# Softmax over rows with stores moved to another DMA queue: six of eight stores issued by GpSimd, one packet for each DMA engine's share

## The chip, the cores and the metric

The kernel runs on one core of a Trainium2 chip. The core has several engines that run side by side, each with its own stream of instructions: VectorE (DVE in the profile), ScalarE (ACT), GpSimd (POOL), SyncE (SP) and TensorE, which this kernel doesn't use. Data moves between main memory and the on-chip buffer by DMA. A DMA is issued by an instruction of SP, ACT or POOL, is split over 16 DMA engines, and signals a semaphore when all shares have landed. The metric is the device time of one execution in microseconds (us); lower is better. Between runs of this kernel it varies by about 0.1%.

## The reference: what is computed

A softmax with temperature 0.5 over the last axis of 16 x 1024 rows of 512 numbers:

```python
batch, seq, dim = 16, 1024, 512
x = np.random.randn(batch, seq, dim).astype(np.float32)

def reference(x):
    temp = 0.5
    x_scaled = x / temp
    x_max = np.max(x_scaled, axis=-1, keepdims=True)
    exp_x = np.exp(x_scaled - x_max)
    return (exp_x / np.sum(exp_x, axis=-1, keepdims=True)).astype(np.float32)
```

The input is 33.55 MB and so is the output. Each is moved once.

## The kernel before

The 16,384 rows are cut into 8 tiles, numbered 0 to 7 here as the variable `c` numbers them. A tile has 128 partitions with `G = 16` rows of 512 float32 each: 32 KB that lie together in main memory for each partition, 4 MB for the tile. `data` has six buffers (`BUFS = 6`): tiles 0 to 5 have one each, tile 6 takes over the buffer of tile 0 and tile 7 that of tile 1. So the load of tile 6 has to wait until the store of tile 0 has landed, and that of tile 7 until the store of tile 1 has.

All loads are issued by SP (line 66). Tile 0 is loaded in two parts, 4 rows and 12 rows of each partition; the others whole. All stores are issued by ACT (line 119), one for each tile. SP's DMAs are queue q1 in the profile and ACT's are q10. Both queues are served by the same 16 DMA engines; each partition's 32 KB of a 4 MB transfer are one packet in the records.

The work goes in 11 blocks (`blocks`): three for tile 0, one each for tiles 1 to 6, two for tile 7. For a block:

- `shift` (lines 68 to 78): DVE takes the maximum of each row, negated (line 74, which waits for the load), and doubles it (line 78). The result is the bias of the exponentials.
- `exponentials` (line 85): ACT computes exp(2x + bias) in place, one instruction for each of the 16 rows of a partition, with the row's sum.
- `scale_vector` (lines 100 and 102): DVE takes the reciprocals of the sums and multiplies all but an eighth of the rows by them, in place.
- `scale_scalar` (line 111): ACT scales the last eighth of the rows, two instructions for a whole tile.
- `store` (line 119): ACT issues the tile's store after its last block.

The order is written out by hand (the schedule is manual), and each engine runs its instructions in that order. In step `i` of the last loop ACT gets the exponentials of block i+1, the scaling of block i and its store. DVE gets the scaling of block i and then the maximum of block i+2. So in the middle of the run, DVE alternates between the multiplication for one tile (line 102) and the maximum of the tile two further on (line 74). A store of tile c comes after the exponentials of tile c+1 in ACT's order. Waits on semaphores are put in by the framework from the data that each instruction touches.

Tile 7's two blocks are the tail: maximum and exponentials of its first half, then of its second half, the two multiplications, and the last store.

Of the kernel before, what the change touches and what calls it, by code (L numbers as in the profile page):

```python
# [1 line left out]

# [4 lines left out]


@with_exitstack
def kernel(  # L10
    ctx: ExitStack,
    tc: tile.TileContext,
    x: bass.AP,
    out: bass.AP,
):
    nc = tc.nc
    fp32 = mybir.dt.float32
    P = nc.NUM_PARTITIONS
    AX = mybir.AxisListType.X
    EXP = mybir.ActivationFunctionType.Exp  # L20
    COPY = mybir.ActivationFunctionType.Copy
    MAX = mybir.AluOpType.max

    D = x.shape[-1]
    xf = x.flatten_outer_dims()
    of = out.flatten_outer_dims()
    N = xf.shape[0]

    G = 16
    C = N // (P * G)
    assert C * P * G == N
    xr = xf.rearrange("(c p g) d -> c p g d", p=P, g=G)
    outr = of.rearrange("(c p g) d -> c p g d", p=P, g=G)
    WHOLE = [(0, G)]
    LOADS = [[(0, 4), (4, G)]] + [WHOLE] * 7
    BLOCKS = [[(0, 4), (4, 8), (8, G)]] + [WHOLE] * 6 + [[(0, 8), (8, G)]]
    STORES = [WHOLE] * 8  # L40
    BMAX = 16
    BUFS = 6

    data = ctx.enter_context(tc.tile_pool(name="data", bufs=BUFS))
    stats = ctx.enter_context(tc.tile_pool(name="stats", bufs=6))

    ctx.enter_context(tc.manual_schedule())


    warm = stats.tile([P, 1], fp32, name="warm", bufs=1)  # L50
    nc.vector.memset(warm, 0.0)  # L51
    nc.scalar.activation(out=warm, in_=warm, func=EXP)  # L52

    chunks = {}
    blocks = [(c, lo, hi) for c in range(C) for lo, hi in BLOCKS[c]]
    n = len(blocks)
    biases, sums, recips = {}, {}, {}

    def load(c):
        if c < BUFS:  # L60
            chunks[c] = data.tile([P, G, D], fp32, name="xt")
        else:
            chunks[c] = chunks[c - BUFS]
        xt = chunks[c]
        for lo, hi in LOADS[c]:
            nc.sync.dma_start(out=xt[:, lo:hi, :], in_=xr[c][:, lo:hi, :])  # L66

    def shift(i):
        c, lo, hi = blocks[i]
        if c not in chunks:  # L70
            load(c)
        b = hi - lo
        negmax = stats.tile([P, BMAX], fp32, name="negmax")
        nc.vector.tensor_reduce(  # L74
            negmax[:, 0:b], chunks[c][:, lo:hi, :], axis=AX, op=MAX, negate=True
        )
        biases[i] = stats.tile([P, BMAX], fp32, name="bias")
        nc.vector.tensor_scalar_mul(biases[i][:, 0:b], negmax[:, 0:b], 2.0)  # L78

    def exponentials(i):  # L80
        c, lo, hi = blocks[i]
        sums[i] = stats.tile([P, BMAX], fp32, name="sums")
        for g in range(hi - lo):
            row = chunks[c][:, lo + g, :]
            nc.scalar.activation(  # L85
                out=row,
                in_=row,
                func=EXP,
                bias=biases[i][:, g : g + 1],
                scale=2.0,  # L90
                accum_out=sums[i][:, g : g + 1],
            )


    def scale_vector(i):
        c, lo, hi = blocks[i]
        b = hi - lo
        k = b - b // 8
        recips[i] = stats.tile([P, BMAX], fp32, name="recip")
        nc.vector.reciprocal(recips[i][:, 0:b], sums[i][:, 0:b])  # L100
        rows = chunks[c][:, lo : lo + k, :]
        nc.vector.tensor_mul(  # L102
            rows, rows, recips[i][:, 0:k].unsqueeze(2).broadcast_to((P, k, D))
        )

    def scale_scalar(i):
        c, lo, hi = blocks[i]
        b = hi - lo
        for g in range(b - b // 8, b):
            row = chunks[c][:, lo + g, :]  # L110
            nc.scalar.activation(  # L111
                out=row, in_=row, func=COPY, scale=recips[i][:, g : g + 1]
            )

    def store(i):
        c, _, end = blocks[i]
        for lo, hi in STORES[c]:
            if hi == end:
                nc.scalar.dma_start(
                    out=outr[c][:, lo:hi, :], in_=chunks[c][:, lo:hi, :]  # L120
                )

    shift(0)
    shift(1)
    exponentials(0)
    for i in range(n):
        if i + 1 < n:
            exponentials(i + 1)
        scale_vector(i)
        scale_scalar(i)  # L130
        if i + 2 < n:
            shift(i + 2)
        store(i)


# [1 line left out]
_INS = ['x']  # L137
_OUTS = [((16, 1024, 512), 'float32')]


# [23 lines left out]
```

## Time and profile before

| quantity | value |
|---|---|
| median of 8 runs | 162.23 us (162.07 to 162.26) |
| the profiled execution's own time | 162.15 us |
| its span (first to last instruction in the profile) | 160.4 us |
| DVE line 74, maximum of a whole tile | 6 times, 8678 ns each |
| DVE line 102, multiplication for a whole tile | 6 times, 7625 ns each |
| ACT line 85, one row's exponential | 128 times, 707 ns each, and 186 ns for its sum |
| idle time of ACT before line 85 | 41.5 us |
| idle time of DVE before line 74 | 9.4 us, all before the first tile's two loads |
| 4 MB stores, issue to landing | median 22.8 us (12.1 to 32.4) |

The median and the profiled execution agree within 0.1 us; the execution's own time is 1.75 us above its span, which is what lies around the instructions. The table's other rows come from the page's groups of instructions, from those groups with shapes kept apart, and from the list of DMA issues.

Issue times of stores and loads, from the timeline, and landing times, which are the issue time plus the time to landing that the list of DMA issues gives for that one DMA:

| tile | load landed | DVE began its maximum (line 74) | store issued | store landed |
|---|---|---|---|---|
| 0 | 5.4 and 12.7 | 5.46 and 12.73 | 45.43 | 69.1 |
| 1 | 22.4 | 24.48 | 58.88 | 88.5 |
| 2 | 32.1 | 37.32 | 75.50 | 107.9 |
| 3 | 42.3 | 53.94 | 92.12 | 120.9 |
| 4 | 56.0 | 70.55 | 108.73 | 130.5 |
| 5 | 75.4 | 87.17 | 125.36 | 140.3 |
| 6 | 94.8 | 103.79 | 132.93 | 149.8 |
| 7 | 114.8 | 120.41 | 147.40 | 159.5 |

The loads of tiles 0 to 5 were all issued in the first 5 us; tile 6's at 69.24, when tile 0's store had landed, and tile 7's at 88.61, when tile 1's had.

### The profile page before, as it was taken

The page shows a single profiled execution, that of the slowest core. Times are in us where ns is not written, and L with a number is a line of the kernel's source. Part 1 is how long each engine was busy: PE and PEld are TensorE (multiplying, and loading weights), DVE is VectorE, ACT ScalarE, POOL GpSimd, SP SyncE. Part 2 cuts the span into 40 slices and gives each one's busy share as a digit, 9 for nine tenths or more (in the row PEclk, how much of TensorE's full clock was granted, in tenths as well). Part 3 has the DMA queues.
Part 4 walks back from the last instruction along what each step waited for, and adds up shares of the span by engine and source line. Part 5 has one row for each costly group of instructions (what it writes and reads, how often), then busy time and mean ns, then how long its engine had stood idle before and what let it go on. Part 6 is the DMA issues. An engine that isn't in the chain of part 4 may idle for free.

```text
span 160.4 us, 402 instructions
## 1 busy us (share of the span) xinstructions
DVE 134.6 (84%) x45; ACT 102.1 (64%) x273; POOL 0.2 (0%) x4
## 2 busy tenths in 40 slices
DVE  0608999999999999999999999999999999957000
ACT  3071549069979963998199909991899891790000
POOL 0000000000000000000000000000000000000000
DMA  5999999999999999999999999999999999999993
GB/s 182 472 392 523 392 392 515 401 392 492 417 400 392 392 433 474 400 417 490 400 392 515 400 392 501 409 392 458 458 392 441 474 392 417 499 392 400 515 392 139
DMA packets 2450, 67.13 MB, mean 419 GB/s; under 512 B 272, under 2 KB 272, under 8 KB 272
## 3 DMA queue, kind: packets, MB, share of 16 engines
q1 hardware_dynamic: 1296, 33.56, 49.3%
q10 hardware_dynamic: 1152, 33.55, 48.5%
q14 instruction: 2, 0.02, 0.0%
HBM read 33.55 MB, written 33.55 MB: 418 GB/s over the span
## 4 chain that ended last, share of the span: by engine, by line
DVE 80%; DMA 7%; ACT 4%; issue 0%; SPq 0%
DVE negmax L74 42%; DVE xt L102 36%; DMA xt<-in_x_dram 7%; ACT xt L85 4%; DVE bias L78 1%; DVE recip L100 1%; SPq L66 0%
## 5 line engine op out<-in xcount | busy, mean ns | idle before, releaser
L85 ACT ACTIVATE xt<-xt,bias 128x512 f32<-128x512 f32 x128 | 90.4, 707 | 41.5 <-DVE bias L78 41.1
L74 DVE TENSOR_REDUCE negmax<-xt 128x16 f32<-128x8192 f32 (+2 forms) x11 | 69.9, 6352 | 9.4 <-DMA xt<-in_x_dram 9.4
L102 DVE TENSOR_TENSOR xt<-xt,recip 128x7168 f32<-128x7168 f32 (+2 forms) x11 | 62.0, 5637 | 0.4
L85 ACT ACTIVATION_READ_ACCUMULATOR xt<-xt,bias 128x1 f32 x128 | 23.8, 186 | 0.0
L111 ACT ACTIVATE xt<-xt,recip 128x512 f32<-128x512 f32 x15 | 9.9, 706 | 0.0
L100 DVE RECIPROCAL recip<-sums 128x16 f32<-128x16 f32 (+2 forms) x11 | 2.4, 218 | 1.8 <-ACT xt L85 1.8
L78 DVE TENSOR_SCALAR bias<-negmax 128x16 f32<-128x16 f32 (+2 forms) x11 | 1.9, 172 | 0.4
L52 ACT ACT_TABLE_LOAD x1 | 1.3, 1283 | 0.7 <-PEq L148 0.7
L51 DVE MEMSET warm<- 128x1 f32 x1 | 0.1, 59 | 0.8 <-PEq L148 0.8
L52 ACT ACTIVATE warm<-warm 128x1 f32<-128x1 f32 x1 | 0.2, 203 | 0.0
L148 POOL MEMSET const-bfloat16-1.0<- 128x1 bf16 x1 | 0.1, 102 | 0.0
L148 POOL MEMSET const-uint8-127<- 128x1 uint8 x1 | 0.1, 102 | 0.0
L148 POOL MEMSET const-float32-0.0<- 128x1 f32 x1 | 0.1, 99 | 0.2 <-issue 0.2
L148 POOL MEMSET const-float32-1.0<- 128x1 f32 x1 | 0.1, 99 | 0.0
## 6 DMA issues: line engine op xcount, KB each, us to landing
out_dram<-xt ACTq DMA_DIRECT2D x8, 4096.0 KB, 22.8
xt<-in_x_dram SPq DMA_DIRECT2D x7, 4096.0 KB, 30.1
xt<-in_x_dram SPq DMA_DIRECT2D x1, 3072.0 KB, 11.6
xt<-in_x_dram SPq DMA_DIRECT2D x1, 1024.0 KB, 4.7
```

The costliest lines, as they stand in the source:

```text
L51: nc.vector.memset(warm, 0.0)
L52: nc.scalar.activation(out=warm, in_=warm, func=EXP)
L74: nc.vector.tensor_reduce(negmax[:, 0:b], chunks[c][:, lo:hi, :], axis=AX, op=MAX, negate=True)
L78: nc.vector.tensor_scalar_mul(biases[i][:, 0:b], negmax[:, 0:b], 2.0)
L85: nc.scalar.activation(out=row, in_=row, func=EXP, bias=biases[i][:, g : g + 1], scale=2.0, accum_out=sums[i][:, g : g + 1],)
L100: nc.vector.reciprocal(recips[i][:, 0:b], sums[i][:, 0:b])
L102: nc.vector.tensor_mul(rows, rows, recips[i][:, 0:k].unsqueeze(2).broadcast_to((P, k, D)))
L111: nc.scalar.activation(out=row, in_=row, func=COPY, scale=recips[i][:, g : g + 1])
L148: nc = _bacc.Bacc("TRN2", target_bir_lowering=False, num_devices=1)
```

## The change

The stores of tiles 1 to 6 are issued by GpSimd (POOL) instead of ACT, with the argument `single_packet=True`, which asks for one packet for each DMA engine's share of the transfer, here the 8 partitions of 32 KB that one engine moves. The stores of tiles 0 and 7 stay as they were. Nothing else is changed: neither the computation nor the order of DVE's instructions, nor that of ACT's other ones.

```diff
         c, _, end = blocks[i]
         for lo, hi in STORES[c]:
             if hi == end:
-                nc.scalar.dma_start(
-                    out=outr[c][:, lo:hi, :], in_=chunks[c][:, lo:hi, :]
-                )
+
+                if 0 < c < C - 1:
+                    nc.gpsimd.dma_start(
+                        out=outr[c][:, lo:hi, :],
+                        in_=chunks[c][:, lo:hi, :],
+                        single_packet=True,
+                    )
+                else:
+                    nc.scalar.dma_start(
+                        out=outr[c][:, lo:hi, :], in_=chunks[c][:, lo:hi, :]
+                    )
```

In the built program POOL's stream, which had nothing after four small memsets at the start, now holds the six stores one after the other. Each waits for its tile's scaling on DVE and on ACT. The load of tile 7 on SP now waits for the store of tile 1 on POOL's queue.

## The prediction

> **What bounds the kernel now.** I read the page's busy shares and its 40 slices first, then the chain that ended last, then the timeline of DVE with the DMA issues, then the DMA queues in single stretches.
>
> ```profile
> DVE 134.6 (84%) x45; ACT 102.1 (64%) x273; POOL 0.2 (0%) x4
> DMA  5999999999999999999999999999999999999993
> DMA packets 2450, 67.13 MB, mean 419 GB/s; under 512 B 272, under 2 KB 272, under 8 KB 272
> DVE negmax L74 42%; DVE xt L102 36%; DMA xt<-in_x_dram 7%; ACT xt L85 4%; DVE bias L78 1%; DVE recip L100 1%; SPq L66 0%
> ```
>
> Two resources are full at once. The DMA engines are at 9 in every slice but the first and the last. DVE is the chain: it idles 9.4 us for the first loads and 1.8 us near the end, and else runs without a gap until the last store is issued. So a load that comes late is paid in full, as DVE has no spare time to make it up.
>
> The timeline has the deadlines and the tail:
>
> ```profile
> 87.17 8.68 DVE L74 TENSOR_REDUCE negmax<-xt 128x16 f32<-128x8192 f32 x1
> 103.79 8.68 DVE L74 TENSOR_REDUCE negmax<-xt 128x16 f32<-128x8192 f32 x1
> 120.41 4.41 DVE L74 TENSOR_REDUCE negmax<-xt 128x8 f32<-128x4096 f32 x1
> 125.22 7.62 DVE L102 TENSOR_TENSOR xt<-xt,recip 128x7168 f32<-128x7168 f32 x1
> 147.40 0.34 ACTq L119 DMA_DIRECT2D out_dram<-xt  x1
> ```
>
> These are the maxima of tiles 5, 6 and 7, a multiplication that matters below, and the last store's issue. The loads landed at 75.4, 94.8 and 114.8, so the slack of tile 5 is 87.17 - 75.4 = 11.8 us, of tile 6 9.0 us and of tile 7 5.6 us. From tile 7's maximum to the last issue are 147.40 - 120.41 = 27.0 us, and from there to the landing 12.1 us.
>
> Who gets the DMA engines while a load and a store are both there is shown by the queues between 56 and 68 us, when q1 had tile 5's load and q10 tile 0's store:
>
> ```profile
> q1 hardware_dynamic: 81, 2.65, 51.2%
> q10 hardware_dynamic: 80, 2.59, 49.9%
> ```
>
> 81 packets against 80: the two queues take turns packet by packet, and a packet is one partition's 32 KB (2.65 MB / 81). What a transfer costs alone is read from 120 to 137 us, where only stores run and the windows give 432 GB/s: 4.194 MB / 432 GB/s = 9.7 us, 1.2 us for each of an engine's 8 rows.
>
> **The change part by part.** *Removed:* six issues from ACT, 0.34 us each, 2.0 us in all. They come after the exponentials and before a wait for DVE; ACT idles 41.5 us for DVE's bias (page). The only time DVE waits for ACT in the tail (1.8 us at line 100) is set by eight exponentials that begin with DVE's bias at 137.2, and the issue before them was at 132.93. Worth 0; without that cover it would be at most 2.0 us.
>
> *Added:* six issues on POOL, which has 0.2 us of other work, so nothing is queued behind them but the next store. No row of before shows a DMA issued there. Its delay from issue to first byte is bounded by the two nearest rows: the last store landed 12.1 us after its issue and needs 9.7 us alone, so 2.4 us for both ends of it together; the first tile's 1 MB load took 4.7 us and needs 2.4 us alone, so 2.3 us. I take 1.5 us ahead of the data, between 0 and 4. It costs nothing by itself, as loads keep the engines busy meanwhile.
>
> *Moved:* the stores stand in a third queue, and an engine's share is one packet of 8 rows in place of 8 packets. How long a turn such a packet gets isn't in the trace, which has only one-row packets. The bounds: one row in each turn (then sharing is as now, 0 us), or all 8 rows in one turn (9.7 us in which neither a load nor tile 0's store moves). What the rows show is that turns go by packets, so I take the upper one. It then goes like this, with issue times of before and DVE's waits added:
>
> - Tile 1's store, issued at 58.88, begins at 60.4 and holds the engines to 70.1. Tile 0's store, which shared with a load and landed at 69.1, lands 9.7 us later at 78.8. Tile 6's load, issued at 69.24 when that landed, now goes out at 79.
> - Tile 5's load lands at 75.4 now, with half the engines. At 60.4 it has (75.4 - 1 - 60.4) / 2 = 7.0 us of engine time to go (1 us for signalling). From 70.1 it shares with tile 0's store; tile 2's store, issued at 75.50, takes over at 77, so 3.4 us of it get done. The rest follows from 86.7 to 90.3, and it lands at about 91, where 87.2 was needed: DVE is late by 3 to 4 us.
> - Tile 6's load begins at 90.3 and is halted 9.7 us by tile 3's store (issued at 92.12): 90.3 + 9.7 + 9.7 = 109.7, landed 110.5. Needed at 103.8: 6 to 7 us late.
> - Tile 4's store waits for exponentials that wait for tile 5's maximum, so it goes out at 108.7 + 3.5 = 112. Tile 7's load began at 109.7 and is halted too: 109.7 + 19.4 = 129.1, landed 130. Needed at 120.4: 9.6 us late.
>
> A check on the last step, without the steps before it: the engines are busy all the time up to there, and both kernels move the same bytes. If the stores of tiles 3 and 4 go ahead of tile 7's load, that load lands when tile 4's store lands now, at 130.5. DVE is then 130.5 - 120.4 = 10.1 us late. A turn of only 2 to 4 rows gives nearly the same, since the store still overtakes the load: this is why the uncertain turn length matters little above one row.
>
> What follows on the path is unchanged: 27.0 us to the last issue and 12.1 us to the landing. Now tile 6's store lands at 149.8, 2.4 us after the last issue, so some engines begin the last store late. With DVE 10 us later, only stores are left after 130 and that backlog has drained: a gain of 0 to 1.1 us (2.4 less the 1.3 us that issue and signalling would take anyway). I take 0.8. **Sum: 10.1 - 0.8 = +9.3 us.** On the profiled execution: 162.15 + 9.3 = 171.4; it is 0.08 us under the median, so 171.5 against 162.23.
>
> [...]
>
> [...]
>
> **Rivals.**
>
> *Turns stay at one row (the argument has no effect on them).* For it: it isn't shown that a longer packet holds an engine. Against: the turns counted above go by packets. Three queues then share from 60.4 to about 71, tile 5's load gets a third in place of a half. Over 10 us it loses 10 x (1/2 - 1/3) = 1.7 us of engine time, 3.4 us at half rate: it lands at 79, before 87.2. Tile 0's store lands some 2 to 3 us later, so do the next loads: 98 before 103.8, and 118 before 120.4. All in time: 162.2, within 0.3. The point that decides is a load more than 5.6 us late.
>
> *Faster: the stores finish sooner and the loads still come in time.* Then only the backlog ahead of the last store goes, 0.8 to 1.1 us: 161.2. For it: each load's slack is 11.8, 9.0 and 5.6 us. Against: one halt of 9.7 us uses up two of these, and 67.13 MB at 432 GB/s are 155.4 of 160.4 us, so there is no more to win. It needs POOL's stores to be late enough, or their turns short enough, for tile 7's load to go before tile 4's store.
>
> [...]
>
> **How the numbers follow.** Halted loads (168 to 174, by 0 to 4 us of delay at POOL and the sum's rounding): 0.72, and its time is the prediction, 171.5. Turns of one row: 0.11. Faster: 0.07. POOL held up, alone or on top: 0.10. A difference under 0.2% can't be told from none for this kernel. So faster 0.07, same 0.11, slower 0.82. The range leaves out the second and third case and reaches down to the fourth alone and up to it on top: 165 to 176.
>
> **What would show it.** Right: DVE idle before line 74 grows from 9.4 to about 19 us, released by loads, in three waits of some 3 each before tiles 5, 6 and 7; stores from POOL land about 12 us after issue (now up to 32.4); the loads of tiles 5 to 7 take much longer; tile 6's load goes out at about 79; the DMA slices show idle time after 130 us, which they haven't now. Wrong: where both queues have work, equal bytes of loads and of POOL's stores, with no more DVE idle; or stores that begin long after their issue; or multiplications (line 102) longer than 7.62 us. The weakest link is the length of a turn; the next is whether tile 4's store does come ahead of tile 7's load.

## The result, and the profile after

The changed kernel takes 163.82 us (median of 11 runs, 163.09 to 164.58) against 162.23 us (31 runs of the kernel before): 1.0098 times as long, 95% interval 1.0084 to 1.0112. It is slower, but by 1.6 us and not by the 9.3 us of the prediction; the time lies below the predicted range of 165 to 176 us. Its runs spread over 1.5 us where those of before spread over 0.65 us. The profiled execution took 164.10 us, 1.95 us more than that of before, with a span of 162.3 us.

From the page of the changed kernel, the lines that answer to those shown of before:

```profile
DVE 134.6 (83%) x45; ACT 102.0 (63%) x273; POOL 3.5 (2%) x10
DMA  5999899899998999999999999999899899899980
DVE negmax L74 41%; DVE xt L102 36%; DMA xt<-in_x_dram 7%; ACT xt L85 4%; DVE bias L78 1%; DVE recip L100 1%; SPq L66 0%
L74 DVE TENSOR_REDUCE negmax<-xt 128x16 f32<-128x8192 f32 (+2 forms) x11 | 69.9, 6352 | 9.5 <-DMA xt<-in_x_dram 9.5
out_dram<-xt POOLq DMA_DIRECT2D x6, 4096.0 KB, 24.3
```

The page of before has for line 74:

```profile
L74 DVE TENSOR_REDUCE negmax<-xt 128x16 f32<-128x8192 f32 (+2 forms) x11 | 69.9, 6352 | 9.4 <-DMA xt<-in_x_dram 9.4
```

DVE is as busy as before, and its idle time ahead of the maxima (line 74) is 9.5 us against 9.4. So no load came late: the prediction's whole mechanism is absent. A store from GpSimd takes 24.3 us to land (the median of six), not the 12 us of a store that would have the DMA engines to itself.

The timeline has the last multiplication and the last store at nearly the same place as before (the store's issue was at 147.40 there), first the multiplication before, then both after:

```profile
143.43 3.89 DVE L102 TENSOR_TENSOR xt<-xt,recip 128x3584 f32<-128x3584 f32 x1
```

```profile
143.58 3.89 DVE L102 TENSOR_TENSOR xt<-xt,recip 128x3584 f32<-128x3584 f32 x1
147.56 0.34 ACTq L127 DMA_DIRECT2D out_dram<-xt  x1
```

0.16 us of the difference is there (the first load landed that much later). The rest comes after the last issue: this store takes 13.6 us to land, the one of before 12.1. What still runs at the end is shown by the DMA queues from 159 us to the end, first before:

```profile
DMA packets 1, 0.00 MB, mean 0 GB/s; under 512 B 1, under 2 KB 1, under 8 KB 1
q10 hardware_dynamic: 1, 0.00, 0.0%
```

and after:

```profile
DMA packets 3, 0.03 MB, mean 10 GB/s; under 512 B 2, under 2 KB 2, under 8 KB 2
q10 hardware_dynamic: 3, 0.03, 2.3%
```

After 159 us one row of 32 KB is still to be moved: one DMA engine of the 16 is behind the others and everything waits for it. Which one a packet ran on isn't in the records, but they can be strung together into 16 chains, in each of which a packet begins when the one ahead of it ends. In the trace of before this holds within 4 ns at 2429 of 2434 joints, and each chain has 72 rows of loads and 64 of stores; after, the chains have the same numbers within one row. A chain is taken for an engine here. The ends of the chains (us from the start of the span), and the lost time of the last one after 50 us, that is, rows that took longer than the usual 1.213 us and gaps:

```
              15 engines end   last engine ends   its lost time after 50 us
before        158.1 to 158.4   159.2              0.76  (of it 0.55 at 98: gap, then a long row)
after         158.2 to 159.0   160.8              2.31  (+0.39 at 53, +0.63 at 79, +0.10 at 84.5,
                                                         +0.12 at 87, 0.45 at 92 to 93.5, +0.63 at 104.5)
```

In both kernels the engine that ends last is the one with the gaps of 0.3 us, and these are the records of program fetches (queue q14, kind "instruction" on the page, 8 KB and 0.31 us each, at 37.6 and 93.2 us after, 37.5 and 98.1 before). It was the last one before, too, by 0.8 us. So the sum of the profiled executions is: 161.14 against 159.51 us for the last landing, +1.63, of which 2.31 - 0.76 = 1.55 is the lost time on the last engine; and from the last landing to the end of the span 1.19 us against 0.86, +0.33. Together +1.96, where +1.95 was measured.

### The profile page after: what moved, and what is told of

It reads as the page before. It is cut to its first block, busy times and chain, and to the rows that moved or that the text cites. A ratio compares the mean times of both kernels' runs of the same rounds, so it can differ in the third digit from the quotient of the medians.

```text
span 162.3 us, 406 instructions
## 1 busy us (share of the span) xinstructions
DVE 134.6 (83%) x45; ACT 102.0 (63%) x273; POOL 3.5 (2%) x10
## 3 DMA queue, kind: packets, MB, share of 16 engines
q10 hardware_dynamic: 288, 8.39, 12.1%
## 4 chain that ended last, share of the span: by engine, by line
DVE 79%; DMA 7%; ACT 4%; issue 0%; SPq 0%
DVE negmax L74 41%; DVE xt L102 36%; DMA xt<-in_x_dram 7%; ACT xt L85 4%; DVE bias L78 1%; DVE recip L100 1%; SPq L66 0%
## 5 line engine op out<-in xcount | busy, mean ns | idle before, releaser
L121 POOL DMA_DIRECT2D out_dram<-xt x6 | 3.3, 553 | 130.3 <-ACT xt L111 123.1
## 6 DMA issues: line engine op xcount, KB each, us to landing
out_dram<-xt POOLq DMA_DIRECT2D x6, 4096.0 KB, 24.3
```

The costliest lines, as they stand in the source:

```text
L121: nc.gpsimd.dma_start(out=outr[c][:, lo:hi, :], in_=chunks[c][:, lo:hi, :], single_packet=True,)
```

## The experiments

The theories at the start: (A) the end is set by the last of the 16 DMA engines, and GpSimd's stores delay that one; (B) the delays are chance. On the turns (how much one queue moves before the other has its turn) there were two more: the one-packet argument has no effect, or it has one which these rows hide. All times beside the experiments are against runs of the kernel before on the same chip.

### The same kernel again, and without the argument

The first is the changed kernel itself; the second is this:

```diff
-                        single_packet=True,
```

> The changed kernel once more, for a second trace and as the measure for the three kernels beside it. Theory A (the last of the 16 DMA engines sets the end, and GpSimd's stores put delays of about 0.6 us on that one engine): 163.8 us, the last engine again 2 to 3 us behind the others at the end, with delays near GpSimd's stores. Theory B (the delays are fetches of program code or the like, which fall where they fall): the same time, but the delays at other places in this trace.

> The same six stores from GpSimd, without the one-packet argument. If the argument has no effect on 32 KB rows (rows of loads and stores take turns one by one, as in the trace with it): 163.8 us, turns and landings as with it. If the argument does lengthen turns in some way that the trace hides: under 163 us and store landings more than 3 us different.

Measured: 164.26 us (ratio 1.0112, 1.0086 to 1.0137) and 163.59 us (1.0091, 1.0064 to 1.0117). The two can't be told apart. The last engine ended at 161.1 and 160.8 us, the others at 159.2 and 159.1 or before, and its long rows stand at the same places in all three traces: near 79 (+0.95 and +0.45 us), 84.5 (+0.25 and +0.21) and 104.6 us (+0.76 and +0.60). So the places of the delays aren't chance, and the argument isn't the cause. Whether every execution has them isn't shown: all three traces are of executions above 164 us, and the times go down to 163.1.

The trace of the changed kernel shows one thing more about the places. Each of the three long rows is the first one after the last engine's own completion write for a transfer (the 4-byte record that closes each engine's share, 16 for each of the 17 transfers, the 272 packets under 512 B of the page): for the load of tile 5 (79 us), the store of tile 1 (84.5) and that of tile 2 (104.5). The row after its write for the load of tile 6 took the usual 1.213 us, and so did the rows at all these places in the kernel before.

### How long a turn is: rows cut into pieces

In the changed kernel the turns are one row each. From its queues between 108 and 110 us, when tile 7's load and a GpSimd store are both there:

```profile
q0 software_dynamic: 16, 0.52, 60.6%
q1 hardware_dynamic: 16, 0.52, 60.6%
```

But rows of 32 KB can't show a packet of several, if the argument is ignored for them. So the rows of a store were cut into pieces of 4 KB, 64 to an engine's share: on GpSimd with and without the argument, and on Scalar in the kernel before.

```diff
                         in_=chunks[c][:, lo:hi, :],
                         single_packet=True,
+                        max_dma_last_dim=4096,
```

> The six GpSimd stores keep the one-packet argument, but each row of 32 KB is cut into pieces of 4 KB (64 pieces in an engine's share). If a turn is one piece whatever the argument says: beside a load's 32 KB rows a store gets one ninth of an engine, so stores of tiles 1 and 2 land more than 35 us after issue, and the records show single 4 KB pieces between rows of loads. If a turn is a packet and the argument sets it: runs of many pieces, up to 64 (9.7 us), between two rows of a load, tile 7's load up to 10 us late, up to 172 us. On the delays of the last engine: if they go by the number of pieces fetched, they grow several times over, to 170 us and more; if not, they stay at about 2 us.

> The same 4 KB pieces without the argument. If the argument sets the turn, the runs of pieces between rows of loads are shorter than with it and the store landings differ by more than 3 us; if it has no effect, both kernels have the same turns and times within 0.5 us.

> The kernel before, all stores on Scalar, with its rows cut into pieces of 4 KB. It tells pieces from queue. If small pieces alone change the turns: stores on Scalar share as unevenly as GpSimd's (one ninth), and the last engine has no delays of 0.6 us. If 4 KB pieces cost nothing on Scalar and delays only come with GpSimd's queue: 162.2 us, unless a load is late.

Measured: 165.48 us (1.0197, 1.0184 to 1.0211), 165.57 us (1.0201, 1.0175 to 1.0227) and 165.57 us (1.0206, 1.0184 to 1.0227). The queues between 74 and 82 us, when a load and a GpSimd store are both there, with the argument:

```profile
q1 hardware_dynamic: 94, 3.08, 89.1%
q0 software_dynamic: 96, 0.39, 11.9%
```

without it:

```profile
q1 hardware_dynamic: 95, 3.11, 90.0%
q0 software_dynamic: 96, 0.39, 11.9%
```

and Scalar's pieces (79 to 86 us):

```profile
q1 hardware_dynamic: 80, 2.62, 86.6%
q10 hardware_dynamic: 81, 0.33, 11.5%
```

The columns are packets, MB and the share of the engines' time. In each, the counts are equal within two and the bytes are eight to one; in the chains of the single engines, load rows and store pieces alternate one by one in all three stretches. A turn is one piece, whether it has 32 KB or 4 KB, on either queue, with the argument or without. This settles the turn.

The 3.3 us that these three lose are about what an estimate from the pieces gives: a piece of 4 KB takes 0.159 us, so eight of them 1.27 us in place of 1.213. That is 0.06 us for each row, 48 rows of an engine for six stores: 2.8 us, and 3.8 us for eight. Eight times the pieces did not multiply the delays of the last engine, which ended 1.1 to 1.4 us behind the next one. The 1.4 us are those of Scalar's pieces, with no GpSimd store at all, against 0.8 us in the kernel before.

### Which stores

```diff
-                if 0 < c < C - 1:
+                if 0 < c < 4:          # first run: tiles 1 to 3
+                if 3 < c < C - 1:      # second run: tiles 4 to 6
```

> Only the stores of tiles 1 to 3, which share the engines with loads, go through GpSimd (one packet each); those of tiles 4 to 6 are back on Scalar. If the cost comes only while loads are under way: 163.8 us, like all six. If it goes by the number of GpSimd's stores: half of it, 163.0 us. If only the late stores cost: 162.2 us.

> Only the stores of tiles 4 to 6, which mostly run with no load beside them, go through GpSimd. If the cost comes only while loads are under way: 162.2 us. If it goes by the number of GpSimd's stores: 163.0 us. If only the late stores cost: 163.8 us.

Measured: 163.83 us (1.0095, 1.0064 to 1.0127) and 162.65 us (1.0019, 1.0010 to 1.0028). The early run has to be read with care, since it met another wait. From its list of waits:

```profile
DVE negmax L74 <- DMA xt<-in_x_dram: 11.4, 3, 4.8
```

Three waits instead of two: tile 7's load came 2 us late, as loads, GpSimd's store of tile 3 and Scalar's of tile 4 shared the engines in threes (1.15, 2.39 and 1.90 MB of their queues between 109 and 122 us), and the DMA engines then waited for the last store, issued at 149.54. So a late load was paid in full, as the prediction had it, at a fifth of its size; but what made it late was sharing in threes, as in the first rival, and not a long turn. The late run lost 0.3 us, and no row of its last engine was long after the fetch at 98 us. What is left there is at the end: on 15 engines the first row of the last store took 0.2 to 1.0 us longer than 1.213.

### The first and the last store

```diff
-                if 0 < c < C - 1:
+                if c < C - 1:          # tiles 0 to 6
+                if c < C:              # all eight
+                if c < C - 2:          # tiles 0 to 5
+                if 0 < c < C - 2:      # tiles 1 to 5
```

> Tile 0's store goes through GpSimd too, so seven of eight; only the last is Scalar's. On all engines the two rows around 47 to 49 us took some 1 us more than others in both traces, when Scalar's first store began. If that comes with Scalar's queue starting: it is gone, and the time falls to 163.0 us or less. If it comes with any first store: 164 us. If the last engine's delays go by the number of GpSimd's stores: 164.2 us.

> All eight stores on GpSimd, so no queue starts from empty at the end, and the last store pays GpSimd's own time from issue to first byte. If the store ahead covers that time: 162.5 us. If GpSimd's issue is later than the engines come free (its issue took 0.53 us, and the engines are free about 1 us after it): up to 1 us more, 163.5 us. If the late engine's delays come with GpSimd's stores: 164 us.

> GpSimd has the stores of tiles 0 to 5, Scalar those of 6 and 7. Like the run with seven on GpSimd, but with Scalar's queue already at work when the last store is issued. If that run's 1.0 us over the kernel before is the empty queue's start (about 0.6 us) and the longer end after GpSimd's DMAs (about 0.3 us): 162.5 us here. If it is a cost of every GpSimd store: 163.0 us.

> GpSimd has the stores of tiles 1 to 5, Scalar those of 0, 6 and 7, so Scalar's queue still has work when the last store is issued. If the 0.5 to 1 us that the first row of the last store takes longer on most engines comes from a queue that starts from empty: that is gone here. The delays on the one late engine (79 to 105 us) should stay, as those stores are unchanged: 163 to 164.5 us. If it doesn't matter what the queue holds: the first row of the last store is still 0.5 to 1 us long.

Measured, beside the ends of the chains:

```
GpSimd's tiles    time, ratio and interval             15 engines end    last engine ends
0 to 6            163.20, 1.0061 (1.0048 to 1.0073)    159.2 to 159.6    159.7
all               162.78, 1.0035 (1.0021 to 1.0049)    158.9 to 159.3    159.8
0 to 5            162.60, 1.0020 (1.0008 to 1.0032)    158.4 to 159.0    159.0
1 to 5            164.02, 1.0090 (1.0064 to 1.0115)    158.0 to 158.8    161.1
```

The last two differ only in the queue of tile 0's store, and by 1.4 us. For tiles 0 to 5 nothing is left to move near the end (158.9 us on):

```profile
q10 hardware_dynamic: 3, 0.00, 0.1%
```

and for tiles 1 to 5 one row is (from the same time):

```profile
q10 hardware_dynamic: 2, 0.03, 2.1%
```

So the delays are no price of each GpSimd store: six of them from tile 0 on cost 0.36 us in all, five from tile 1 on cost 1.8 us. In the trace with tiles 1 to 5 the long rows are again at 79 (+0.90 us), 84.6 (+0.21) and 104.7 (+0.67); in that with 0 to 5 the engine with the fetch gaps has, after 60 us, only the fetch at 92 us (this trace is of the fastest of its executions, 162.27 us). In the trace with tiles 1 to 5 a second engine has long rows too, at 75.8 (+0.44) and 84.8 us (+0.26), and so in the one without the argument (75.9 and 84.7 us, +0.37 and +0.36). So the delays aren't bound to the engine with the fetches.

What the last store's start costs is measured as well. With tile 6's store on Scalar, no engine's first row of the last store is long in these two traces; with tile 6's on GpSimd, where Scalar's queue had nothing in it when the last store was issued, it took 0.7 to 1.1 us longer on 15 engines in the run with tiles 0 to 6. Between the first row of the table and the third that is 0.6 us of time. With all eight on GpSimd that start is gone too; its last store began after a gap of up to 0.6 us on 14 engines instead.

An empty queue alone doesn't cost this. Scalar's queue was empty too when tile 6's store was issued at 132.97 us (tiles 0 to 5 on GpSimd), and GpSimd's when its first store was issued at 59.31 us in the changed kernel. There the engines still had other rows to move, the new queue's first row began 3.6 to 5.9 us after the issue, and it took 1.213 us. With tiles 0 to 6 on GpSimd, the last store's first row began 1.2 to 1.4 us after the issue on most engines, which by then had nothing else to move. Why it then took longer isn't shown.

### GpSimd's queue in use at all

```diff
     nc.scalar.activation(out=warm, in_=warm, func=EXP)
+    tiny = stats.tile([P, 16], fp32, name="tiny", bufs=1)
+    nc.gpsimd.dma_start(out=tiny, in_=xr[0][:, 0, 0:16])
```

> The kernel before with one more DMA, 8 KB from GpSimd at the very start, whose data isn't used. If a kernel that uses GpSimd's DMA queue at all ends some 0.3 us later (from the last landing to the end of the span 1.2 in place of 0.9 us): 162.5 us. If the end is longer only by what GpSimd's late stores do: 162.25 us.

Measured: 162.59 us (1.0021, 1.0006 to 1.0036). The last landing was 0.2 us later than before, and from there to the end of the span it was 0.98 us, where before had 0.86 and the kernels with five or more large GpSimd stores have 1.13 to 1.36. So a small DMA costs as much as expected in all, but only a third of it at the expected place. The stretch at the end grows with the number of GpSimd's large stores: 0.88 us in the trace with one (below), 1.0 us in the two with three, and 1.13 us or more with five and up. That it comes with any use of the queue isn't shown, and the trace with one store speaks against it.

### Three queues at once, or the change of queue

```diff
-                if 0 < c < C - 1:
+                if 0 < c < C - 2:
+                    if c == 1:
+                        nc.gpsimd.memset(chunks[0][:, 0:1, 0:1], 0.0)
```

and, for the other, GpSimd for tile 0 alone:

```diff
-                if 0 < c < C - 1:
+                if c == 0:
```

> As the run with GpSimd for tiles 1 to 5 and Scalar for 0, 6 and 7 (164.0 us), but GpSimd's first store waits until the store of tile 0 has landed (a one-element write into tile 0's buffer, which the load of tile 6 overwrites later, stands ahead of it). So there is never a load, a Scalar store and a GpSimd store under way together between 64 and 71 us. If that stretch with three queues, and the order of transfers that it leaves, is what delays the late engine: 162.6 us. If the change of queue after tile 0 is enough: 164 us as before.

> The hand-over the other way round: only tile 0's store is GpSimd's, all others are Scalar's. If three queues at once, whichever comes first, delay the late engine: 163.5 to 164.5 us. If it takes GpSimd's stores beside loads after a store of Scalar's: 162.6 us (0.3 us for the longer end alone).

Measured: 165.97 us (1.0233, 1.0210 to 1.0257) and 163.20 us (1.0063, 1.0033 to 1.0094; nine runs of 162.39 to 164.66, without a tenth at 165.14). Neither is clean. In the first, the store of tile 1 and the load of tile 6 both had to wait for tile 0's landing, so at 70 us both queues started with nothing or next to nothing in them. From the queues between 70 and 78 us:

```profile
DMA packets 93, 2.52 MB, mean 315 GB/s; under 512 B 16, under 2 KB 16, under 8 KB 16
```

315 GB/s, where busy engines move 432 (120 to 137 us, before and after): by an estimate from these two some 2 us are lost there in the mean over the engines, which is more than the wait was to save. Beside that its last engine still had long rows at 97 (+0.18) and 109.5 us (+0.68), without a stretch of three queues. The second, in which GpSimd has one store only, has the largest spread of times of all, and in its trace the load queue also ran dry: tile 6's load was issued at 76.1, tile 5's ended at 77 to 78, and on several engines the rows around 82 to 84 us took 0.4 to 0.6 us longer. In that trace six engines ended late together (159.6 to 159.7 us), not one. So, as far as these two traces show, delays come without three queues at once and with a single GpSimd store. With whole rows, two store queues used one after the other while loads are under way go with delays in either order; one store queue for that stretch goes without the long rows at 79 to 105 us (before, tiles 0 to 5, 0 to 6, all eight). This is what goes together, not a cause.

## Why the prediction was wrong

**What bounds the kernel.** Half right. DVE's chain and the DMA engines are both full, as the profile said. What the page can't show, because it takes 16 engines together, is that the end hangs on a single one: before, that engine ended at 159.2 us and the next at 158.4. The mean share of 9 in every slice hid this.

**The step that failed:** "What the rows show is that turns go by packets, so I take the upper one." The records of before have one packet for each row, so that packet, row and turn couldn't be told apart there; the bounds given were 0 and 9.7 us, and the upper one was taken. Measured: a turn is one row, or one 4 KB piece, also where the argument asks for one packet. The bound of 0 holds, and with it the first rival. That an engine stays with one queue for more than a row was the author's assumption, and no run shows it: the counts were 96 pieces against 94 rows with the argument, 96 against 95 without. Nor do the records show one packet for an engine's share: the changed kernel has 864 packets for its six GpSimd stores, 144 for each, and the kernel before has as many for each of Scalar's (1152 for eight).

**The halted loads.** None. DVE waited 9.5 us for loads where about 19 were forecast. The first rival's landings, worked out from shares of a third and of a half, came close: 79, 98 and 118 us for the loads of tiles 5, 6 and 7, measured 79.3, 100.1 and 120.0. The last was needed at 120.56, so 0.6 us of slack were left of 5.6. The run with GpSimd's stores of tiles 1 to 3 went over that edge by 2 us.

**The first rival's time** (162.2, within 0.3) was still 1.6 us short. Missing were the last engine's delays (1.55 us in the profiled execution) and the longer end of the span (0.33 us). No term of the prediction could hold them: it had one DMA rate for 16 engines, and nothing after the last landing.

**ACT's issues** saved nothing, as said. **The tail's gain** of 0.8 us didn't come: without a late DVE the store of tile 6 is still under way at the last issue, and the last store's first rows, from a Scalar queue empty by then, took up to 0.65 us longer.

**POOL held up by DVE**, that is, a store's issue that waits for a multiplication, has 0.10 in the forecast, and both ends of the range (165 and 176) come from it. No run shows such a wait. In the changed kernel POOL's issues took 0.53 us each (the first 0.67), tile 5's at 125.77, inside the multiplication at 125.36, as much as the others; the multiplications kept their 7.62 us.

**Two terms of the halted loads.** POOL's 1.5 us from issue to data was an estimate: its first store's first rows began 5.2 to 5.9 us after the issue at 59.31. The 1 us for signalling is shown by no run; in the trace of before the last landing came 0.35 us after the last record (159.51 against 159.16). The 1.3 us for issue and signalling at the last store is in that trace: 0.98 us from the issue to its first row at 148.38, and the same 0.35 us.

**Faster** was given 0.07 with the backlog ahead of the last store as its gain; none of the variants reached it.

**What stays open.** Why the last engine is delayed when the stores change queue isn't shown; the two runs made for that each brought delays of their own. Nor is it shown why single runs of the changed kernel lie between 163.1 and 164.6 us: all its traces are of executions above 164 us. A run at 163.1 would fit a kernel without the delays but with the slow start and the longer end, as the one with tiles 0 to 6 (163.2), but no trace of such a run shows it.

## What to carry to other kernels

When transfers share DMA engines, count the turns in the records while two queues are at work, and don't build on a turn length that the trace can't tell from another: cutting rows into 4 KB pieces showed it at once. With its DMA engines full, this kernel ended with its slowest one (159.2 us against 158.4 of the next, 160.8 against 159.0 after the change), which a mean over 16 hides; look at what still moves in the last microseconds. What the runs of this kernel speak for is to keep the stores on one queue while loads are under way, and to give the last store a queue that still has work when it is issued: of the variants here that moved whole rows to GpSimd, the two that did cost 0.4 and 0.5 us and the others 0.9 us and more, but none was faster than Scalar's queue alone, as the bytes and the engines are the same. The exception is the run that moved only late stores, which changed queue when the loads were nearly done and lost 0.3 us.

## What the hardware showed that was not expected

- The DMA engines switched queue after each piece: 96 pieces of 4 KB to 94 rows of 32 KB between 74 and 82 us, so the load's queue moved eight times the bytes of the store's (3.08 against 0.39 MB). With rows on both, between 108 and 110 us in the changed kernel, the counts were 16 to 16 and the bytes equal (0.52 MB each). The size of the pieces set the share of a queue there.
- A 4 KB piece takes 0.159 us, eight of them 5% more than a 32 KB row (1.213 us).
- A queue that started from empty cost time only in some places. The last store's first row, with nothing else to move, took up to 1.1 us longer at 148 us where Scalar's queue was empty, and two queues that started at once lost some 2 us, by the estimate from 315 against 432 GB/s. GpSimd's start at 59 us and Scalar's at 133 us, with other rows to move meanwhile, cost nothing: 1.213 us for the first row, 3.6 to 5.9 us after the issue. At the start of the first store (47 to 49 us) load rows are long on all engines, by 0.5 to 1.0 us in the kernel before.
- The long rows that delay the last engine, up to 0.95 us each, are the first ones after its completion write for a transfer (79, 84.5 and 104.5 us in the changed kernel); in the kernel before, the rows at these places take 1.213 us.
- One engine lost 0.31 us at each program fetch, with a row after it that took 0.11 to 0.37 us longer, and ended last by 0.8 us in the kernel before, by 1.8 us after.
- From the last landing to the end of the span it takes 0.86 us before, 0.88 us with one large GpSimd store, 1.0 us with three, and 1.13 to 1.36 us with five or more.
